# A third Strassen pair in the first MLP product of a two-layer encoder, with four conversion buffers and another order of the conversions

## The chip, the cores and the metric

The kernel runs on one core of a Trainium2 chip. The metric is the device time of one execution in microseconds. The engines are named as the profile names them: PE is TensorE (matmuls; PEld its weight loads), DVE is VectorE, ACT is ScalarE, POOL is GpSimd, SP is SyncE, which here issues the weight loads from memory.

## The reference

A trunk of two layers on 256 rows of width 2048, in float32. Each layer is an attention half (two kinds of attention, gated and merged) and an MLP half; the change touches the MLP half and, through one rule of order, the products in front of it.

```
for l in range(DEPTH):                                   # DEPTH = 2
    u = rmsnorm(x, norm_mix[l]);  proj = u @ w_in[l]     # 2048 x 8256
    ...                                                  # MLA and neighbourhood attention, gates
    x = x + merged @ w_out[l]                            # 2048 x 2048
    h = rmsnorm(x, norm_mlp[l]) @ w_ff1[l]               # 2048 x 8192
    x = x + jnp.square(jax.nn.relu(h)) @ w_ff2[l]        # 8192 x 2048
return rmsnorm(x, norm_final)
```

## The kernel before, in words

**Precision by halves.** Every float32 operand of a large product is cut in two: `hi` is a copy in the format that the matmuls take (float32r), made by ACT, and `lo` is the source minus `hi`, made by DVE (`parts`, lines 173 to 179). A product is then three matmuls: hi x hi, hi x lo, lo x hi. For weights this is work for each 1 MB piece that is loaded; for the activations it is done once, and the two parts lie in slots (`pair`).

**A product call, `gemm_s`.** It multiplies the 256 x 2048 activations by 1024 columns of a weight matrix. The 2048 rows are cut into 8 *row pairs* of 256 rows. For each, SP loads one raw tile `raw` (128 x 2048, three buffers), and a pair is either *plain* or *Strassen*. A plain pair is 8 products of three 128x512 matmuls, with one conversion of 2048 columns. A Strassen pair is 7 products of three (in Winograd's form): DVE first builds four sums of the weights' blocks (`sums`, lines 465, 468, 469), then three raw blocks (1536 columns) and the four sums (2048 columns) are converted. The activations need four sums too (`sums_of`, lines 364 to 367), made once for each pair that is Strassen. The results of the products stand in eight PSUM banks; at the end of a call DVE adds them up into four result tiles (line 476, the evacuation) and calls `evac`.

**What is Strassen where.** `MIXED` and `MERGED` name the pairs of the gate products and of the output product (1, 2, 3, visited in the order 0, 4, 1, 5, 2, 6, 3, 7), `FIRST` those of the first MLP product, `SECOND` those of the second (both visited from 0 to 7).

**The MLP half.** It runs in four blocks of 2048 hidden columns. A block is two calls of the first product (`w_ff1`), whose results go through ReLU, 16 transposes and a square into new activations (`turned_pair`, lines 391 to 413), and two calls of the second (`w_ff2`), whose results POOL adds into `x` by accumulating DMAs (line 870); the last block has one such call, and its other half by plain products (`gemm_a`). So there are 16 calls of the first product and 14 of the second in the two layers. The transposes and conversions of new activations are generators that are advanced by ticks between the products of the next call; `drain()`, at a call's first Strassen pair, finishes all of them.

**What sets the order.** A scheduler orders each engine's instructions when the program is built, by its own model of time; each engine then works strictly in that order, and waits where an input or a free buffer is late. The tile pools set which buffers there are: `raws` (3), `hi` and `lo` (3 each in the MLP half, 8 KB a partition), `sums` (1), and 52 slots of 2 KB for activations and results.

Of the kernel before, what the change touches and what calls it, by code (L numbers as in the profile page):

```python
# [33 lines left out]
F32 = mybir.dt.float32  # L34
F32R = mybir.dt.float32r
AF = mybir.ActivationFunctionType
ALU = mybir.AluOpType
AX = mybir.AxisListType

P = 128  # L40
S = 256
# [17 lines left out]

NSLOT, SMALL, RBUFS, HBUFS = 52, 8, 3, 4


FIRST, SECOND = (3, 5), (2, 4, 6)


MIXED, MERGED = (1, 2, 3), (1, 2, 3)
# [7 lines left out]
def trunk(ctx: ExitStack, tc: tile.TileContext, x, w_in, w_uq, w_ukv, rpb, w_o_mla, w_o_na,  # L76
          w_out, w_ff1, w_ff2, gains, gain_fin, cos, sin, turns, halves, mask, out):
    nc = tc.nc
    const = ctx.enter_context(tc.tile_pool(name="const", bufs=1))
    slots = ctx.enter_context(tc.tile_pool(name="slots", bufs=NSLOT))  # L80
    keep = ctx.enter_context(tc.tile_pool(name="keep", bufs=2))
    raws = ctx.enter_context(tc.tile_pool(name="raws", bufs=RBUFS))
    psum = ctx.enter_context(tc.tile_pool(name="psum", bufs=8, space=bass.MemoryType.PSUM))

    tmp = wpool = spool = None
    hbufs, smalls, strips = HBUFS, SMALL, False

    def bank():
        return psum.tile([P, 512], F32, tag="bank", name="bank", bufs=8)
# [7 lines left out]
    def wide():  # L97
        return slots.tile([P, 512], F32, tag="slot", name="wide")
# [30 lines left out]
    def tick():  # L129
        clock[0] += 1  # L130
        for i, (ready, gen) in enumerate(pending):
            if ready <= clock[0]:
                advance(i)
                return
        if queued and clock[0] - clock[1] >= SPACING:
            clock[1] = clock[0]
            pending.append((clock[0], queued.pop(0)))
            advance(len(pending) - 1)
# [9 lines left out]
    def drain():  # L148
        while pending or queued:
            if pending:  # L150
                clock[0] = max(clock[0], pending[0][0])
            tick()
# [20 lines left out]
    def parts(src):  # L173

        hi, lo = (wpool.tile([P, 2048 if strips else 1024], F32R, tag=tag, name=tag,
                             bufs=3 if strips else hbufs)[:, :src.shape[-1]] for tag in ("hi", "lo"))
        nc.scalar.copy(hi, src)  # L177
        nc.vector.tensor_tensor(lo, src, hi.bitcast(F32), op=ALU.subtract)  # L178
        return hi, lo
# [109 lines left out]

    def rows_of(col):  # L290

        dg = [keep.tile([P, P], F32, tag="diag", name="diag", bufs=4) for _ in range(2)]
        for t in range(2):
            nc.vector.tensor_scalar_mul(dg[t], ident, col[:, t:t + 1])
        yield 8
        pb = abank()
        for t in range(2):
            nc.tensor.matmul(pb[:, t * P:(t + 1) * P], ones, dg[t], start=True, stop=True)
        row = keep.tile([P, S], F32, tag="rrow", name="rrow", bufs=4)
        nc.vector.tensor_copy(row, pb[:, :S])  # L300
        return row

# [7 lines left out]
    class Norm:  # L310
# [5 lines left out]
        def add(self, t):  # L316
            if self.acc is None:
                self.acc = tmp.tile([P, S], F32, tag="acc", name="acc", bufs=2)
                nc.scalar.activation(self.acc, t, AF.Square)
                return  # L320
            sq = small()
            nc.scalar.activation(sq, t, AF.Square)
            nc.vector.tensor_tensor(self.acc, self.acc, sq, op=ALU.add)

        def scales(self):

            ps = abank()
            for t in range(2):
                nc.tensor.matmul(ps[:, 2 * t:2 * t + 2], self.acc[:, t * P:(t + 1) * P], ones[:, :2],
                                 start=True, stop=True)  # L330
            v = keep.tile([P, 2], F32, tag="var", name="var", bufs=2)
            nc.vector.tensor_copy(v, ps[:, 0:4:2])
            self.col = root(v, self.width, "col")
            self.row = yield from rows_of(self.col)
# [80 lines left out]
    def gemm_s(w, c0, get, order, pairs, evac):  # L415

        b, count, total = {}, {}, {i: 0 for i in range(1, 9)}
        for j in order:  # L420
            for i in (range(1, 8) if j in pairs else (2, 3, 4, 8)):
                total[i] += 3 if j in pairs else 6

        def mm(i, x, y):
            if i not in b:
                b[i], count[i] = bank(), 0
            count[i] += 1
            nc.tensor.matmul(b[i], x, y, start=count[i] == 1, stop=count[i] == total[i])  # L428

        def products(*todo):  # L430
            for n, (i, ah, al, wh, wl) in enumerate(todo):
                mm(i, ah, wh)
                mm(i, al, wh)
                if n % 2:
                    tick()
            for i, ah, al, wh, wl in todo:
                mm(i, ah, wl)

        def cut(src):
            out, step = [], 2048 if strips else 1024  # L440
            for c in range(0, src.shape[-1], step):
                hi, lo = parts(src[:, c:min(c + step, src.shape[-1])])
                out += [(hi[:, i:i + 512], lo[:, i:i + 512]) for i in range(0, hi.shape[-1], 512)]
            return out

        first = next(j for j in order if j in pairs)
        for j in order:
            raw = raws.tile([P, 2048], F32, tag="raw", name="raw", bufs=RBUFS)
            nc.sync.dma_start(raw.rearrange("p (k n) -> p k n", n=1024),
                              w[2 * j * P:(2 * j + 2) * P, c0:c0 + 1024].rearrange("(k p) n -> p k n", p=P))  # L450
            if j not in pairs:
                ws = cut(raw)
                ah, al = get(j)
                products(*((i, ah[2 * k + t], al[2 * k + t], *ws[2 * k + side])
                           for k in range(2) for i, t, side in ((2, 0, 1), (3, 0, 0), (4, 1, 1), (8, 1, 0))))
                continue
            if j == first:
                drain()
            if strips:
                whole_ts = spool.tile([P, 2048], F32, tag="sums", name="sums", bufs=1)  # L460
                ts = whole_ts[:, :1024], whole_ts[:, 1024:]
            else:
                ts = [tmp.tile([P, 1024], F32, tag="pp", name="sums", bufs=2) for _ in range(2)]
            t1, t3, t2, t4 = (s[:, i:i + 512] for s in ts for i in range(0, 1024, 512))
            nc.vector.tensor_tensor(ts[0].rearrange("p (a n) -> p a n", a=2),  # L465
                                    raw[:, :512].rearrange("p (a n) -> p a n", a=1).to_broadcast([P, 2, 512]),
                                    raw[:, 512:1536].rearrange("p (a n) -> p a n", a=2), op=ALU.subtract)
            nc.vector.tensor_tensor(t2, raw[:, 1024:1536], t1, op=ALU.subtract)
            nc.vector.tensor_tensor(t4, raw[:, 1536:], t2, op=ALU.subtract)  # L469
            w11, w22, w21 = cut(raw[:, 512:])  # L470
            w1, w3, w2, w4 = cut(whole_ts) if strips else cut(ts[0]) + cut(ts[1])
            (a11, _, a12, a22, s1, s2, s3, s4), (l11, _, l12, l22, r1, r2, r3, r4) = get(j)
            products((1, a11, l11, *w11), (2, a12, l12, *w21), (3, s4, r4, *w22), (5, s1, r1, *w1),
                     (7, s3, r3, *w3), (6, s2, r2, *w2), (4, a22, l22, *w4))
        r11, r22, r12, r21 = (wide() for _ in range(4))
        add = lambda o, a, c: nc.vector.tensor_tensor(o, a, c, op=ALU.add)  # L476
        nc.scalar.copy(r11, b[1])
        add(r22, r11, b[6])
        add(r12, r22, b[5])
        add(r21, r22, b[7])  # L480
        add(r22, r21, b[5])
        add(r12, r12, b[3])
        add(r11, r11, b[2])
        add(r22, r22, b[8])
        add(r21, r21, b[4])
        evac({(0, 1): r11, (0, 0): r12, (1, 1): r21, (1, 0): r22})
# [171 lines left out]
    for l in range(DEPTH):  # L658
        half_a = ExitStack()
        hbufs, smalls, strips = HBUFS, SMALL, False  # L660
        wpool = half_a.enter_context(tc.tile_pool(name="wpool", bufs=4, reuse_waits="tile"))
        tmp = half_a.enter_context(tc.tile_pool(name="tmp", bufs=2, reuse_waits="tile"))
# [67 lines left out]

        mixed = blocks(xg, xs4, MIXED)
        gemm_s(wi, C_GB, mixed, ORDER, MIXED, gate(part, 0))
        local(0)
        local(1)
        gemm_s(wi, C_GB + 1024, mixed, ORDER, MIXED, gate(part, 1))
        for g in range(2):
            gemm_s(wi, C_GA + g * 1024, mixed, ORDER, MIXED, gate(other, g))
# [63 lines left out]
        last = l == DEPTH - 1  # L801
        half_b = ExitStack()
        strips = True
        spool = half_b.enter_context(tc.tile_pool(name="spool", bufs=1, reuse_waits="tile"))
        wpool = half_b.enter_context(tc.tile_pool(name="wpool2", bufs=4, reuse_waits="tile"))
        tmp = half_b.enter_context(tc.tile_pool(name="tmp2", bufs=2, reuse_waits="tile"))
        mlp = RowNorm()
# [151 lines left out]
```

## Time and profile before

| | |
|---|---|
| median of 3 runs | 2630.33 us (2630.33 to 2630.65) |
| profiled execution | 2630.92 us, its span 2629.1 us |
| granted PE clock, mean | 0.998 |
| PE / PEld busy | 2599.1 us (99%) / 2183.3 us (83%) |
| DVE / ACT / POOL busy | 2116.7 us (81%) / 1457.8 us (55%) / 97.2 us (4%) |
| read from HBM | 492.18 MB |

A time with the span's start as zero is called by its microsecond: the first layer's MLP half runs from 626.7 on. "Busy" of a row is the union of its instructions' times, "idle before" the time its engine stood still just ahead of them, with what ended it. In a timeline, neighbours of one line are merged, and the idle time stands in brackets.

### The profile page before, as it was taken

The numbers are of one execution on the slowest core, as the hardware profiler recorded it, in microseconds if no ns is written. First come the engines' busy times: TensorE is split into PE (matmuls) and PEld (weight loads), VectorE is DVE, ScalarE is ACT, GpSimd is POOL, SyncE is SP. The second block draws the span as 40 slices with busy tenths as digits, with TensorE's granted clock in tenths as the row PEclk, the third lists the DMA queues.
The fourth block names the chain that finished last, engine by engine and source line by source line (L and its number), as shares of the span: only waits on it lengthen the run. The fifth ranks groups of instructions, "written<-read, shape, count | busy, mean of one in ns | idle before, by whom it ended". The sixth has DMA issues, their size and how long they took to land.

```text
span 2629.1 us, 32272 instructions
## 1 busy us (share of the span) xinstructions
PE 2599.1 (99%) x12498; PEld 2183.3 (83%) x12498; DVE 2116.7 (81%) x2496; ACT 1457.8 (55%) x1719; POOL 97.2 (4%) x117
## 2 busy tenths in 40 slices
PE   8999999999999999999999999999999999999998
PEld 7888888878888888888888888888788888888886
DVE  6678789789888888888667787896998888888885
ACT  6555556546655545546545555564566555455553
POOL 1100000000000010000001000000000000100000
PEclk9999999999999999999999999999999999999999
DMA  7555555555567485675565555644555765756744
GB/s 243 182 159 192 192 195 170 162 179 192 200 198 242 160 244 199 199 241 178 190 195 174 173 180 190 207 146 160 188 196 192 217 210 195 244 196 198 259 160 148
DMA packets 175258, 508.97 MB, mean 194 GB/s; under 512 B 13696, under 2 KB 18176, under 8 KB 175104
## 3 DMA queue, kind: packets, MB, share of 16 engines
q1 hardware_dynamic: 166192, 490.08, 55.7%
q0 software_dynamic: 8768, 16.78, 3.3%
q8 instruction: 98, 1.61, 0.2%
q14 instruction: 56, 0.46, 0.1%
q10 hardware_dynamic: 144, 0.04, 0.0%
HBM read 492.18 MB, written 2.10 MB: 188 GB/s over the span
## 4 chain that ended last, share of the span: by engine, by line
PE 76%; issue 19%; DVE 2%; ACT 1%; POOL 1%; DMA 0%; SPq 0%; POOLq 0%; DVEq 0%; ACTq 0%
PE bank L428 47%; PE bank L244 8%; PE bank L279 7%; PE bank L248 4%; PE bank L283 3%; PE bank L223 1%; PE bank L398 1%; DVE lo L178 1%; PE bank L252 1%; PE bank L224 1%; PE bank L254 1%; PE bank L253 1%; POOL xt L870 1%; PE bank L558 0%; ACT hi L177 0%
## 5 line engine op out<-in xcount | busy, mean ns | idle before, releaser
L428 PE MATMUL bank<-hi,pair 128*128 128x512 f32 x5156 | 1269.8, 390 | 7.0 <-ACT hi L177 6.2
L428 PEld LDWEIGHTS bank<-hi,pair 128*128 128x128 f32 x5156 | 964.9, 188 | 210.6 <-ACT hi L177 9.9
L177 ACT CAST hi<-raw 128x2048 fp32r<-128x2048 f32 (+3 forms) x416 | 630.0, 1534 | 449.1 <-PE bank L428 323.0
L178 DVE TENSOR_TENSOR lo<-raw,hi 128x2048 fp32r<-128x2048 f32 (+3 forms) x416 | 751.0, 1817 | 94.7 <-ACT hi L177 61.5
L428 PE MATMUL bank<-lo,pair 128*128 128x512 f32 x2578 | 677.4, 389 | 0.0
L428 PEld LDWEIGHTS bank<-lo,pair 128*128 128x128 f32 x2578 | 483.7, 188 | 100.2
L178 DVE TENSOR_TENSOR lo<-sums,hi 128x2048 fp32r<-128x2048 f32 (+1 forms) x134 | 254.6, 1909 | 176.3 <-ACT hi L177 118.5
L177 ACT CAST hi<-sums 128x2048 fp32r<-128x2048 f32 (+1 forms) x134 | 214.8, 1603 | 290.3 <-DVE sums L469 187.4
L202 DVE TENSOR_TENSOR lo<-raw,hi 128x1024 fp32r<-128x1024 f32 (+1 forms) x224 | 268.7, 1205 | 121.9 <-ACT hi L201 114.2
L201 ACT CAST hi<-raw 128x1024 fp32r<-128x1024 f32 (+1 forms) x224 | 230.0, 1036 | 208.6 <-PE bank L279 84.8
L244 PE MATMUL bank<-hi,pair 128*128 128x512 f32 x1024 | 259.6, 390 | 0.0
L244 PEld LDWEIGHTS bank<-hi,pair 128*128 128x128 f32 x1024 | 190.6, 188 | 38.9
L476 DVE TENSOR_TENSOR wide<-wide,bank 128x512 f32<-128x512 f32 x336 | 216.1, 680 | 4.5 <-PE bank L428 4.1
L279 PE MATMUL bank<-pair,hi 128*128 128x512 f32 x768 | 203.2, 397 | 4.5 <-ACT hi L201 3.2
L279 PEld LDWEIGHTS bank<-pair,hi 128*128 128x128 f32 x768 | 136.3, 190 | 26.9 <-ACT hi L201 3.6
L248 PE MATMUL bank<-lo,pair 128*128 128x512 f32 x512 | 142.8, 392 | 0.0
L465 DVE TENSOR_TENSOR sums<-raw 128x1024 f32<-128x1024 f32 x110 | 134.1, 1219 | 5.7 <-DMA raw<-in_w_ff 5.1
L283 PEld LDWEIGHTS bank<-pair,lo 128*128 128x128 f32 x768 | 106.9, 190 | 8.7
L283 PE MATMUL bank<-pair,lo 128*128 128x256 f32 x768 | 111.6, 283 | 0.0
L248 PEld LDWEIGHTS bank<-lo,pair 128*128 128x128 f32 x512 | 95.2, 188 | 18.9
L408 DVE TENSOR_TENSOR pair<-wide,pair 128x512 fp32r<-128x512 f32 x108 | 72.4, 686 | 13.9 <-ACT pair L407 13.9
L870 POOL DMA_DIRECT2D xt<-wide x48 | 42.3, 968 | 977.0 <-DVE wide L476 702.6
(131 smaller groups left out, 1727.8 us busy)
## 6 DMA issues: line engine op xcount, KB each, us to landing
raw<-in_w_ff SPq DMA_DIRECT2D x256, 1024.0 KB, 5.2
raw<-in_w_in SPq DMA_DIRECT2D x124, 1024.0 KB, 5.1
raw<-in_w_out SPq DMA_DIRECT2D x32, 1024.0 KB, 5.3
raw<-in_w_o_na SPq DMA_DIRECT2D x16, 1024.0 KB, 5.0
raw<-in_w_o_mla SPq DMA_DIRECT2D x16, 1024.0 KB, 5.0
xt<-wide POOLq DMA_DIRECT2D x48, 256.0 KB, 6.8
raw<-in_w_ukv SPq DMA_DIRECT2D x8, 1024.0 KB, 5.6
raw<-in_w_uq SPq DMA_DIRECT2D x8, 768.0 KB, 4.6
```

What stands on the lines that cost most here:

```text
L177: nc.scalar.copy(hi, src)
L178: nc.vector.tensor_tensor(lo, src, hi.bitcast(F32), op=ALU.subtract)
L201: nc.scalar.copy(hi, src)
L202: nc.vector.tensor_tensor(lo, src, hi.bitcast(F32), op=ALU.subtract)
L244: nc.tensor.matmul(ps[t], a, wh[:, k], start=k0 + k + i == 0, stop=False)
L248: nc.tensor.matmul(ps[t], sides(have(acts, k0 + k), t)[0], wl[:, k], start=False, stop=k0 + k == nk - 1)
L279: nc.tensor.matmul(ps[m], wh[:, k, m * P:(m + 1) * P], have(acts, k0 + k), start=k0 + k == 0, stop=False)
L283: nc.tensor.matmul(ps[m][:, :S], wl[:, k, m * P:(m + 1) * P], have(acts, k0 + k)[:, :S], start=False, stop=k0 + k == nk - 1)
L408: nc.vector.tensor_tensor(lw, src, h.bitcast(F32), op=ALU.subtract)
L428: nc.tensor.matmul(b[i], x, y, start=count[i] == 1, stop=count[i] == total[i])
L465: nc.vector.tensor_tensor(ts[0].rearrange("p (a n) -> p a n", a=2), raw[:, :512].rearrange("p (a n) -> p a n", a=1).to_broadcast([P, 2, 512]),
L476: add = lambda o, a, c: nc.vector.tensor_tensor(o, a, c, op=ALU.add)
```

## The change

It does these things:

- `FIRST` goes from (3, 5) to (2, 4, 6): three of the eight row pairs of each first-product call are Strassen. The activations' sums are then made for pairs 2, 4 and 6.
- `hi` and `lo` have four buffers each in the MLP half instead of three, and `sums` moves from a pool of its own into theirs.
- The conversion of a Strassen pair's raw blocks is issued behind the last of the sums (`tc.issue_after`), in all products.
- To make room, one slot goes (51), two small tiles (`diag`, `rrow`) move from a lasting pool to the halves' own, and the scratch for POOL's DMAs is halved.

```diff
-NSLOT, SMALL, RBUFS, HBUFS = 52, 8, 3, 4
-FIRST, SECOND = (3, 5), (2, 4, 6)
+NSLOT, SMALL, RBUFS, HBUFS = 51, 8, 3, 4
+FIRST, SECOND = (2, 4, 6), (2, 4, 6)
...
         hi, lo = (wpool.tile([P, 2048 if strips else 1024], F32R, tag=tag, name=tag,
-                             bufs=3 if strips else hbufs)[:, :src.shape[-1]] for tag in ("hi", "lo"))
+                             bufs=hbufs)[:, :src.shape[-1]] for tag in ("hi", "lo"))
...
-        dg = [keep.tile([P, P], F32, tag="diag", name="diag", bufs=4) for _ in range(2)]
+        dg = [tmp.tile([P, P], F32, tag="diag", name="diag", bufs=4) for _ in range(2)]
...
-        row = keep.tile([P, S], F32, tag="rrow", name="rrow", bufs=4)
+        row = tmp.tile([P, S], F32, tag="rrow", name="rrow", bufs=4)
...
-                whole_ts = spool.tile([P, 2048], F32, tag="sums", name="sums", bufs=1)
+                whole_ts = wpool.tile([P, 2048], F32, tag="sums", name="sums", bufs=1)
...
-            nc.vector.tensor_tensor(t4, raw[:, 1536:], t2, op=ALU.subtract)
-            w11, w22, w21 = cut(raw[:, 512:])
+            final = nc.vector.tensor_tensor(t4, raw[:, 1536:], t2, op=ALU.subtract)
+            with tc.issue_after(final.ins):
+                w11, w22, w21 = cut(raw[:, 512:])
...
-        spool = half_b.enter_context(tc.tile_pool(name="spool", bufs=1, reuse_waits="tile"))
...
-    nc = bacc.Bacc("TRN2", target_bir_lowering=False, num_devices=1, dynamic_dma_scratch_size=8192)
+    nc = bacc.Bacc("TRN2", target_bir_lowering=False, num_devices=1, dynamic_dma_scratch_size=4096)
```

In the program's order, PE has 48 matmuls of 128x512 fewer (32 with a hi of the weights, 16 with a lo). DVE has 16 more of each of the three sums, 16 conversions of 2048 raw columns fewer, 16 of 1536 and 16 of the sums more, and in each layer one more set of the activations' sums and its lo; ACT's conversions change alike. The orders of SP and POOL are the same. From line 470 on, the lines of the changed kernel are one higher, so its evacuation is L477.

First place: DVE in the first call of the first product in the second MLP block of layer 0 (the call at 800.30). Before, from the middle of its first Strassen pair (`sums_7206`, pair 3) through its second (`sums_7275`, pair 5); `lo_7246` is pair 4:

```order
L468 TENSOR_TENSOR sums_7206<-raw_7204,sums_7206 128x512
L469 TENSOR_TENSOR sums_7206<-raw_7204,sums_7206 128x512
L178 TENSOR_TENSOR lo_7211<-raw_7204,hi_7210 128x1536
L178 TENSOR_TENSOR lo_7215<-sums_7206,hi_7214 128x2048
L465 TENSOR_TENSOR sums_7275<-raw_7273 128x1024
L178 TENSOR_TENSOR lo_7246<-raw_7243,hi_7245 128x2048
L468 TENSOR_TENSOR sums_7275<-raw_7273,sums_7275 128x512
L178 TENSOR_TENSOR lo_7280<-raw_7273,hi_7279 128x1536
L469 TENSOR_TENSOR sums_7275<-raw_7273,sums_7275 128x512
L178 TENSOR_TENSOR lo_7284<-sums_7275,hi_7283 128x2048
```

The same stretch now, from the end of pair 2's sums (`sums_7192`) through pair 4's (`sums_7261`); `lo_7232` is pair 3:

```order
L469 TENSOR_TENSOR sums_7192<-raw_7190,sums_7192 128x512
L178 TENSOR_TENSOR lo_7197<-raw_7190,hi_7196 128x1536
L477 TENSOR_TENSOR wide_7110<-wide_7110,bank_6861 128x512
L477 TENSOR_TENSOR wide_7112<-wide_7112,bank_6858 128x512
L178 TENSOR_TENSOR lo_7201<-sums_7192,hi_7200 128x2048
L465 TENSOR_TENSOR sums_7261<-raw_7259 128x1024
L178 TENSOR_TENSOR lo_7232<-raw_7229,hi_7231 128x2048
L468 TENSOR_TENSOR sums_7261<-raw_7259,sums_7261 128x512
L469 TENSOR_TENSOR sums_7261<-raw_7259,sums_7261 128x512
L178 TENSOR_TENSOR lo_7266<-raw_7259,hi_7265 128x1536
L178 TENSOR_TENSOR lo_7270<-sums_7261,hi_7269 128x2048
```

The raw lo (1536 columns) of the second Strassen pair stood between its sums and now stands behind the last of them; the first Strassen pair comes one plain pair earlier, so the last two additions of the call before (L477) now stand between its two conversions.

Second place: DVE at the opening of layer 0's MLP, the first call of the first product (the call at 626.70), around the residual additions into `xt` that the transposes of the activations wait for. Before, with `sums_5981` the first Strassen pair:

```order
L465 TENSOR_TENSOR sums_5981<-raw_5979 128x1024
L825 TENSOR_TENSOR xt0_87<-xt0_87,wide_5797 128x512
L825 TENSOR_TENSOR xt0_87<-xt0_87,wide_5799 128x512
L476 TENSOR_TENSOR wide_5798<-wide_5798,bank_5492 128x512
L476 TENSOR_TENSOR wide_5800<-wide_5800,bank_5489 128x512
L468 TENSOR_TENSOR sums_5981<-raw_5979,sums_5981 128x512
L825 TENSOR_TENSOR xt1_88<-xt1_88,wide_5798 128x512
L178 TENSOR_TENSOR lo_5986<-raw_5979,hi_5985 128x1536
L825 TENSOR_TENSOR xt1_88<-xt1_88,wide_5800 128x512
L469 TENSOR_TENSOR sums_5981<-raw_5979,sums_5981 128x512
```

Now, with `sums_5957`:

```order
L468 TENSOR_TENSOR sums_5957<-raw_5955,sums_5957 128x512
L825 TENSOR_TENSOR xt0_87<-xt0_87,wide_5794 128x512
L825 TENSOR_TENSOR xt0_87<-xt0_87,wide_5796 128x512
L477 TENSOR_TENSOR wide_5795<-wide_5795,bank_5489 128x512
L477 TENSOR_TENSOR wide_5797<-wide_5797,bank_5486 128x512
L469 TENSOR_TENSOR sums_5957<-raw_5955,sums_5957 128x512
L178 TENSOR_TENSOR lo_5962<-raw_5955,hi_5961 128x1536
L825 TENSOR_TENSOR xt1_88<-xt1_88,wide_5795 128x512
L825 TENSOR_TENSOR xt1_88<-xt1_88,wide_5797 128x512
L178 TENSOR_TENSOR lo_5966<-sums_5957,hi_5965 128x2048
```

The last sum (L469) moved ahead of the raw lo and ahead of the second pair of residual additions, which now stand behind both.

More of the change, by code (lines that the diff above doesn't have):

```diff
@@ L83, in trunk @@
     psum = ctx.enter_context(tc.tile_pool(name="psum", bufs=8, space=bass.MemoryType.PSUM))
-    tmp = wpool = spool = None
+    tmp = wpool = None
     hbufs, smalls, strips = HBUFS, SMALL, False
```

## The prediction

> **What bounds the kernel now.** I read the page first: the busy shares, the granted clock, and the chain that ended last.
>
> ```profile
> span 2629.1 us, 32272 instructions
> PE 2599.1 (99%) x12498; PEld 2183.3 (83%) x12498; DVE 2116.7 (81%) x2496; ACT 1457.8 (55%) x1719; POOL 97.2 (4%) x117
> PEclk9999999999999999999999999999999999999999
> PE 76%; issue 19%; DVE 2%; ACT 1%; POOL 1%; DMA 0%; SPq 0%; POOLq 0%; DVEq 0%; ACTq 0%
> ```
>
> TensorE (PE) is busy for 99% of the span at full clock, and the chain is PE and its issue for 95%. A busy PE is not yet PE at its pace, so I read the pace from the timeline, at the end of the second first-product call of the first MLP block, columns: start, duration, then the instructions merged.
>
> ```profile
> 710.14 3.79 PE L428 MATMUL bank<-hi,pair 128*128 128x512 f32 x16
> 713.77 1.98 PE L428 MATMUL bank<-lo,pair 128*128 128x512 f32 x8
> 715.58 0.62 PE L428 MATMUL bank<-hi,pair 128*128 128x512 f32 x2
> ```
>
> From 710.14 to 713.77 there are 16 matmuls, from 713.77 to 715.58 eight: 0.227 us and 0.226 us each. I use 0.227. The weights' conversion is what could break this pace, so I cut the layer at its matrix-product calls; the columns are the stretch, its length, then busy time (instructions) of PE, PEld, DVE, ACT, POOL, clock, DMA share, GB/s.
>
> ```profile
> 539.40:583.50 44.10, 43.13 (x192) 35.15 (x193) 40.64 (x40) 24.13 (x20) 0.00 (x0) 1.00 0.60 190
> 583.50:626.70 43.20, 43.20 (x200) 36.03 (x199) 41.34 (x42) 28.33 (x34) 0.00 (x0) 1.00 0.61 204
> 626.70:671.70 45.00, 44.73 (x204) 36.36 (x203) 39.24 (x43) 27.96 (x33) 0.69 (x1) 1.00 0.55 190
> 671.70:715.60 43.90, 43.90 (x204) 36.59 (x203) 37.71 (x37) 26.31 (x25) 0.00 (x0) 1.00 0.64 213
> 715.60:758.80 43.20, 43.20 (x200) 36.04 (x199) 35.70 (x37) 26.62 (x25) 0.00 (x0) 1.00 0.49 160
> 758.80:800.30 41.50, 41.50 (x184) 34.35 (x183) 35.16 (x29) 19.61 (x12) 3.59 (x4) 1.00 0.77 236
> 800.30:842.50 42.20, 42.20 (x188) 34.94 (x187) 34.64 (x30) 20.41 (x12) 3.55 (x4) 1.00 0.80 255
> 842.50:886.40 43.90, 43.90 (x204) 36.59 (x202) 36.08 (x35) 26.19 (x25) 0.00 (x0) 1.00 0.54 187
> ```
>
> The first two are the two calls of the attention's output product, then come first product (two calls), second product (two calls), and the next block's first product (two calls). The first-product call at 800.30 has 186 matmuls and takes 42.20 us; the second-product call before it has three Strassen pairs, so 183 matmuls, and takes 41.50 us. Both are their matmul counts times 0.227 us (42.2 and 41.5): nothing waits. The calls with 43.2 and 43.9 carry 16 transposes more, 1.7 us or 0.11 each. So PE sets the time call by call, and one call already runs in the form the change gives the first product. Only the stretch at 626.70 is longer than its like (45.00 against 43.90): 1.1 us of waiting at the opening of a layer's MLP. The waits of PE from 530 to 720 us name it, and the waits of a whole steady stretch (758.8 to 971.1) show what the converters wait for (total us, times, longest):
>
> ```profile
> PE bank L428 <- ACT hi L177: 2.0, 2, 1.1
> PE bank L428 <- ACT pair L407: 0.3, 1, 0.3
> ...
> ACT hi L177 <- DVE sums L469: 42.9, 9, 6.4
> ACT hi L177 <- PE bank L428: 39.6, 22, 7.3
> DVE lo L178 <- ACT hi L177: 26.6, 15, 2.5
> ```
>
> In the steady stretch PE has no row among the waiters; ScalarE (ACT) and VectorE (DVE) wait for each other and for PE to free buffers.
>
> **The change part by part.** Durations, one row for each form (busy us in total, mean ns of one, idle before):
>
> ```profile
> L178 DVE TENSOR_TENSOR lo<-raw,hi 128x2048 fp32r<-128x2048 f32 x202 | 459.9, 2286 | 55.8 <-ACT hi L177 39.1 <-PE bank L428 11.5 <-ACT pair L166 3.9
> L177 ACT CAST hi<-raw 128x2048 fp32r<-128x2048 f32 x202 | 383.7, 1913 | 203.3 <-PE bank L428 142.3 <-DMA raw<-in_w_ff 35.0 <-PE bank L244 16.0
> L178 DVE TENSOR_TENSOR lo<-sums,hi 128x2048 fp32r<-128x2048 f32 x86 | 197.1, 2292 | 140.2 <-ACT hi L177 118.0 <-PE bank L428 22.1
> L177 ACT CAST hi<-sums 128x2048 fp32r<-128x2048 f32 x86 | 164.3, 1911 | 233.2 <-DVE sums L469 183.5 <-PE bank L428 49.7
> L178 DVE TENSOR_TENSOR lo<-raw,hi 128x1536 fp32r<-128x1536 f32 x86 | 150.8, 1754 | 18.2 <-ACT hi L177 11.7 <-PE bank L428 5.7
> L465 DVE TENSOR_TENSOR sums<-raw 128x1024 f32<-128x1024 f32 x110 | 134.1, 1219 | 5.7 <-DMA raw<-in_w_ff 5.1 <-DMA raw<-in_w_in 0.3
> L177 ACT CAST hi<-raw 128x1536 fp32r<-128x1536 f32 x86 | 127.6, 1484 | 161.7 <-PE bank L428 129.1 <-DMA raw<-in_w_ff 24.4 <-DMA raw<-in_w_out 6.4
> L469 DVE TENSOR_TENSOR sums<-raw,sums 128x512 f32<-128x512 f32 x110 | 75.4, 685 | 0.8
> L468 DVE TENSOR_TENSOR sums<-raw,sums 128x512 f32<-128x512 f32 x110 | 75.2, 684 | 0.1
> L408 DVE TENSOR_TENSOR pair<-wide,pair 128x512 fp32r<-128x512 f32 x108 | 72.4, 686 | 13.9 <-ACT pair L407 13.9
> L364 DVE TENSOR_TENSOR wide<-wide 128x128 f32<-128x128 f32 x40 | 11.3, 283 | 0.0
> ```
>
> *The third Strassen pair.* A plain pair is 8 products of 3 matmuls, a Strassen pair 7 of 3. Two layers x four blocks x two calls = 16 calls lose 3 matmuls each: 48 x 0.227 = 10.9 us off PE, all of it on the path. (By the two calls compared above: 16 x 0.70 = 11.2, the same within the windows' edges.)
>
> [...]
>
> What the pair adds: on DVE 1219 + 684 + 685 + 1754 + 2292 in place of 2286 = 4.35 us a call by durations. Neighbours overlap a little on DVE:
>
> ```profile
> 843.48 1.88 DVE L476 TENSOR_TENSOR wide<-wide,bank 128x512 f32<-128x512 f32 x3
> ```
>
> Three of about 0.68 us take 1.88, so one instruction more costs some 0.08 us less than its duration; with four more that is 4.0 us a call, 64 us in all. On ACT 1484 + 1911 - 1913 = 1.5 us a call. Where does it lie? A steady block (715.6 to 886.4) has 35.70 + 35.16 + 34.64 + 36.08 = 141.6 us of DVE in 170.8; it gets 149.6 in 169.4, 88%. Its fullest first-product call goes from 36.08 to 40.1 of 43.2. ACT stays near 28 of 43. I price this at nothing: the cover is PE's own stream. If the cover fails, each call can show up to the 4.0 us (ACT's 1.5 runs beside it).
>
> *The opening of a layer's MLP.* There the cover is thin. The call at 626.70 has 39.24 us of DVE, gets the 4.0 and one more Strassen form of the activations (4 x 0.28 + 0.69 = 1.8 by durations, about 1.4 by pitch; of the three pairs two now fall in this call): 44.6 against 45.00 - 0.7 = 44.3. The call before has 41.34 of 43.20, the call after goes to 41.7 of 43.2. So DVE falls behind by a fraction and catches up later. From above: 4.0 + 1.4 = 5.4 us a layer if all of it shows. From below: -1.1 if the present wait goes, since the fourth buffer lets conversion run ahead. It is nearest to its own ledger, 44.6 - 44.3 = 0.3, and I take 0.5 a layer, +1.0 in all.
>
> *Four buffers.* hi and lo are allocated one chunk of 2048 further ahead, which the rows of ACT waiting for a PE bank bear on: 39.6 us in the steady stretch, none of it on PE's path. It gains only where PE waits: the first output-product call (44.10, with 8 transposes of 0.11 us it should take 42.4, so 1.7 us) and the opening. From -1.7 to +1.7 a layer; I take 0, as nothing in that call's amount of work changes.
>
> *Raw lo behind the sums.* The last sum and then ACT's hi of the sums come one 1.75 us conversion earlier; the raw lo comes 1.4 us later (L468, L469). PE uses the raw lo only after 14 products with hi, 3.2 us into the pair, and today it is not waited for. The raw buffer is freed when both the last sum and the raw lo are done, the same total as before. What hangs on it is the next load on SyncE's queue:
>
> ```profile
> raw<-in_w_ff SPq DMA_DIRECT2D x256, 1024.0 KB, 5.2
> xt<-wide POOLq DMA_DIRECT2D x48, 256.0 KB, 6.8
> ...
> SPq L449 <- DVE lo L178: 158.6, 32, 13.1
> ```
>
> SyncE waits for lo in any case; a load lands 5.2 us after issue, a pair lasts 4.8 to 5.4 us on PE, and three raw buffers give some 15 us. Cost 0.
>
> *Memory paid for it.* 51 slots for 52 while the third pair holds two more: the activations' 22, the hidden's 22 and a result's 4 make 48, so 3 are left where 6 were; a turned pair wants two for a moment. The scratch for GpSimd's DMAs is halved; its accumulating DMAs land in 6.8 us and come four to a call of over 41 us. The rows moved to the tmp pool change no instruction. All 0, at worst a wait of the order of the 1.1 us above at a few places.
>
> Sum: -10.9 + 1.0 = -9.9 us. The profiled run took 2630.92 with a span of 2629.1, so 2621.0 for it; the median 2630.33 lies 0.6 lower, which gives 2620.4.
>
> **The rivals.**
>
> *DVE becomes the bound in the first product.* DVE works in order; behind a waiting evacuation (L476) stand the next lo, the sums for ACT, and through them PE. In a steady block DVE idles 29.2 us now; if those idles (ACT's hi, banks not yet complete) cannot shrink, the added 4.0 us a call show on PE. It is slower than now from 0.68 us of PE waiting a call (10.9/16), by over 0.2% from 1.0 us. At half, 2.0 a call: 2630.3 - 10.9 + 32 = 2651. For it: 93% in the fullest call. Against it: the output call at 583.50 runs with 41.34 of 43.20 and no wait, and the second product has the form already. Chance 0.08.
>
> *The openings eat the gain.* The full 5.4 us a layer: 2630.3 - 10.9 + 10.8 = 2630, no change; a half leaves -5.5, the edge of 0.2%. For it: the one wait today is there. Chance 0.11 for within 0.2%, 0.07 for a smaller gain that still counts.
>
> *The waits of today go too.* Fourth buffer and order remove 1.1 and 1.7 a layer: 2630.3 - 10.9 - 5.6 = 2613.8. The first wait of the output product is for a first conversion that no buffer hurries, so 0.08.
>
> *Something else spaces PE's stream,* such as the weight loads, and a matmul less saves only that.
>
> ```profile
> L428 PEld LDWEIGHTS bank<-hi,pair 128*128 128x128 f32 x5156 | 964.9, 188 | 210.6 <-ACT hi L177 9.9 <-ACT pair L407 1.4 <-DVE pair L408 0.8
> ```
>
> At 188 ns the 48 bring 9.0 us: 2622.3. Against it: the two compared calls differ by 0.70 us for 3 matmuls, not by 0.56. Chance 0.01. [...]
>
> *The change doesn't do what it says:* the program's order has 48 products fewer on PE, and the sums ahead of the raw lo; no chance left for that.
>
> **How the numbers follow.** The forecast case has 0.65, its own range 2618 to 2624. What a measurement can tell from no change is about 0.2%, 5.3 us. Faster: 0.65 + 0.07 + 0.08 + 0.01 = 0.81; same: 0.11; slower: 0.08. The range 2616 to 2627 leaves out the DVE-bound case (0.08), most of the openings' case (0.07) and part of the best case (0.04).
>
> **What would show it.** PE's L428 rows have 5124 and 2562 matmuls, at the same mean. Each later first-product call is 0.7 us shorter (41.5, 43.2) with no wait row of PE; DVE's busy total is some 65 us higher and its share near 83 to 84%. A row of PE waiting for L177 or L408 in the later blocks would show the DVE rival; stretches over 45 us at each layer's opening the second. Wrong would be above all a first product at 42.2 or more with DVE near 100% of it.

## The result and the profile after

The changed kernel takes 2616.69 us (median of 4 runs, 2615.81 to 2617.43), the kernel before in the same comparison 2630.33 (2630.01 to 2630.65): a ratio of 0.9948 with a 95% interval of 0.9931 to 0.9965, so 13.6 us less where 9.9 were forecast. The page of its profiled execution (2616.59 us):

```profile
span 2614.8 us, 32295 instructions
PE 2588.5 (99%) x12450; PEld 2173.8 (83%) x12450; DVE 2183.3 (83%) x2570; ACT 1483.6 (57%) x1737; POOL 101.2 (4%) x117
PE 88%; issue 8%; DVE 2%; ACT 1%; DMA 0%; POOL 0%; SPq 0%; POOLq 0%; DVEq 0%; ACTq 0%
L428 PE MATMUL bank<-hi,pair 128*128 128x512 f32 x5124 | 1284.2, 390 | 4.1 <-ACT hi L177 3.9
```

There are 48 matmuls fewer (12450 against 12498), DVE is busy for 66.6 us more, and a matmul's mean is as before. The windows below are the same eight calls as in the prediction (output product twice, then two first-product and two second-product calls, then the next block's first product):

```profile
538.80:581.30 42.50, 42.50 (x191) 35.29 (x192) 42.10 (x42) 25.14 (x21) 0.00 (x0) 1.00 0.64 208
581.30:624.60 43.30, 43.30 (x200) 36.00 (x199) 40.34 (x42) 27.99 (x34) 0.00 (x0) 1.00 0.58 196
624.60:668.70 44.10, 43.96 (x201) 35.85 (x201) 41.61 (x50) 28.23 (x34) 2.93 (x1) 1.00 0.52 181
668.70:711.90 43.20, 43.20 (x200) 36.03 (x199) 40.68 (x38) 28.47 (x26) 0.00 (x0) 1.00 0.62 206
711.90:755.30 43.40, 43.40 (x201) 35.99 (x200) 38.38 (x44) 26.99 (x26) 0.00 (x0) 1.00 0.56 179
755.30:796.80 41.50, 41.50 (x185) 34.37 (x184) 39.17 (x32) 21.32 (x13) 3.66 (x4) 1.00 0.87 277
796.80:838.20 41.40, 41.40 (x184) 34.30 (x183) 36.04 (x30) 20.37 (x13) 3.54 (x4) 1.00 0.74 226
838.20:881.50 43.30, 43.30 (x200) 35.96 (x199) 38.25 (x37) 27.60 (x25) 0.00 (x0) 1.00 0.57 192
```

The later first-product calls go from 42.2 to 41.4 or 41.5 and from 43.9 to 43.3, as the count of matmuls says. Two stretches gain that were not meant to: the first output-product call (44.1 to 42.5) and the MLP's opening (45.0 to 44.1). The calls' lengths by the starts of the matmuls, both layers added, give the account: output product -2.9, openings -1.9, the 14 other first-product calls -0.59 to -0.68 each or -9.0, the second product's calls +0.7 in all. That is -13.1 of the 14.3 between the two profiled executions; the rest is spread.

PE's waits from 528 to 720 us, and what the converters wait for in the steady stretch (755.3 to 966.3):

```profile
PE bank L428 <- ACT hi L177: 0.8, 1, 0.8
```
```profile
ACT hi L177 <- DVE sums L469: 37.8, 10, 4.9
ACT hi L177 <- PE bank L428: 21.4, 15, 3.3
```

Of PE's two waits before (2.0 us), the one of 1.13 us at 539.40, ahead of the output product's first matmul, is still there with 0.81 at 538.79, and the one of 0.82 at 563.86 is gone. ACT waits for a bank 21.4 us where it was 39.6. The wait that went is seen in the output product, here before the change; a timeline's columns are start, duration, instruction, and the idle time ahead of it:

```profile
557.03 1.22 DVE L465 TENSOR_TENSOR sums<-raw 128x1024 f32<-128x1024 f32 x1
558.17 1.75 DVE L178 TENSOR_TENSOR lo<-raw,hi 128x1536 fp32r<-128x1536 f32 x1
560.17 0.68 DVE L468 TENSOR_TENSOR sums<-raw,sums 128x512 f32<-128x512 f32 x1
561.10 0.68 DVE L469 TENSOR_TENSOR sums<-raw,sums 128x512 f32<-128x512 f32 x1
561.89 1.91 ACT L177 CAST hi<-sums 128x2048 fp32r<-128x2048 f32 x1 [0.95 <-DVE sums L469]
563.86 4.37 PE L428 MATMUL bank<-hi,pair 128*128 128x512 f32 x16 [0.82 <-ACT hi L177]
```

and after it:

```profile
555.13 1.22 DVE L465 TENSOR_TENSOR sums<-raw 128x1024 f32<-128x1024 f32 x1
556.60 0.68 DVE L468 TENSOR_TENSOR sums<-raw,sums 128x512 f32<-128x512 f32 x1
557.53 0.68 DVE L469 TENSOR_TENSOR sums<-raw,sums 128x512 f32<-128x512 f32 x1
558.13 1.75 DVE L178 TENSOR_TENSOR lo<-raw,hi 128x1536 fp32r<-128x1536 f32 x1
558.32 1.92 ACT L177 CAST hi<-sums 128x2048 fp32r<-128x2048 f32 x1 [0.95 <-DVE sums L469]
```

PE's wait hangs on a chain through three engines: DVE's last sum (L469), ACT's `hi` of the sums, PE. Before, the raw `lo` of 1.75 us stood inside this chain. Now L469 starts 2.40 us behind the start of L465 instead of 4.07, the `hi` starts 3.19 behind it instead of 4.86, and PE has no wait there. That the order alone does this, and not the buffers, is what the experiments have to show.

### The profile page after: what moved, and what is told of

Read it like the earlier page. It is cut to its first block, busy times and chain, and to the rows that moved or that the text cites. A ratio compares the mean times of both kernels' runs of the same rounds, so it can differ in the third digit from the quotient of the medians.

```text
span 2614.8 us, 32295 instructions
## 1 busy us (share of the span) xinstructions
PE 2588.5 (99%) x12450; PEld 2173.8 (83%) x12450; DVE 2183.3 (83%) x2570; ACT 1483.6 (57%) x1737; POOL 101.2 (4%) x117
## 4 chain that ended last, share of the span: by engine, by line
PE 88%; issue 8%; DVE 2%; ACT 1%; DMA 0%; POOL 0%; SPq 0%; POOLq 0%; DVEq 0%; ACTq 0%
PE bank L428 59%; PE bank L244 8%; PE bank L279 7%; PE bank L248 4%; PE bank L283 3%; PE bank L223 2%; PE bank L398 1%; PE bank L224 1%; PE bank L252 1%; PE bank L254 1%; PE bank L253 1%; DVE lo L178 1%; PE bank L559 1%; PE bank L496 0%; ACT hi L177 0%
## 5 line engine op out<-in xcount | busy, mean ns | idle before, releaser
L428 PE MATMUL bank<-hi,pair 128*128 128x512 f32 x5124 | 1284.2, 390 | 4.1 <-ACT hi L177 3.9
L428 PEld LDWEIGHTS bank<-hi,pair 128*128 128x128 f32 x5124 | 958.0, 188 | 204.8 <-ACT hi L177 5.6
L178 DVE TENSOR_TENSOR lo<-raw,hi 128x2048 fp32r<-128x2048 f32 (+3 forms) x416 | 741.8, 1796 | 77.3 <-ACT hi L177 50.9
L177 ACT CAST hi<-raw 128x2048 fp32r<-128x2048 f32 (+3 forms) x416 | 622.8, 1517 | 307.5 <-PE bank L428 163.3
L428 PE MATMUL bank<-lo,pair 128*128 128x512 f32 x2562 | 697.6, 390 | 0.0
L428 PEld LDWEIGHTS bank<-lo,pair 128*128 128x128 f32 x2562 | 479.7, 188 | 99.3
L177 ACT CAST hi<-sums 128x2048 fp32r<-128x2048 f32 (+1 forms) x150 | 244.9, 1638 | 292.3 <-DVE sums L469 167.8
L178 DVE TENSOR_TENSOR lo<-sums,hi 128x2048 fp32r<-128x2048 f32 (+1 forms) x150 | 290.8, 1947 | 98.6 <-ACT hi L177 58.7
L244 PE MATMUL bank<-hi,pair 128*128 128x512 f32 x1024 | 261.0, 391 | 0.0
L477 DVE TENSOR_TENSOR wide<-wide,bank 128x512 f32<-128x512 f32 x336 | 214.9, 679 | 6.5 <-PE bank L428 6.4
L465 DVE TENSOR_TENSOR sums<-raw 128x1024 f32<-128x1024 f32 x126 | 153.6, 1219 | 6.2 <-DMA raw<-in_w_ff 4.8
L248 PE MATMUL bank<-lo,pair 128*128 128x512 f32 x512 | 141.6, 391 | 0.0
L407 ACT CAST pair<-wide 128x512 fp32r<-128x512 f32 x110 | 68.2, 620 | 56.8 <-DVE wide L366 54.5
L469 DVE TENSOR_TENSOR sums<-raw,sums 128x512 f32<-128x512 f32 x126 | 86.6, 687 | 2.1
```

The source lines that it names most:

```text
L244: nc.tensor.matmul(ps[t], a, wh[:, k], start=k0 + k + i == 0, stop=False)
L248: nc.tensor.matmul(ps[t], sides(have(acts, k0 + k), t)[0], wl[:, k], start=False, stop=k0 + k == nk - 1)
L469: final = nc.vector.tensor_tensor(t4, raw[:, 1536:], t2, op=ALU.subtract)
```

## The experiments

The theories: A, the saved matmuls and the order each bring their part, whatever else is done; B, the fourth buffer carries the gain; C, the order is the condition on which the third pair and the buffers pay at all. For each run the ratio is to the kernel before, with its 95% interval.

**The third pair alone** (before, with one line changed):

```diff
-FIRST, SECOND = (3, 5), (2, 4, 6)
+FIRST, SECOND = (2, 4, 6), (2, 4, 6)
```

> The kernel before with only FIRST = (2, 4, 6): three hi and lo buffers, raw lo where the scheduler puts it. Theory A (the gain is 10.9 us of matmuls plus 3.2 us of waits in the output product that the new order of the conversions takes away; the fourth buffer brings little by itself): the 48 matmuls go and little else, 2619 to 2621 us, each later first-product call 41.5 and 43.3 us, the first output-product call still 44.1 us. Theory B (the fourth buffer is what lets the third pair pay): the first product waits for its hi with three buffers, 0.3 us a call or more, so 2624 us or more. Theory C (the order is what lets it pay): the same as B here.

Measured: 2639.66 us, 1.0036 [1.0024, 1.0049]: 9.2 us slower, with 48 matmuls fewer. That misses theory A's 2619 to 2621 us and fits the 2624 or more of B and C. The steady first-product calls do shorten (42.16 to 41.48), but the openings grow to 48.6 and 47.8 us, the first second-product call of each block from 43.25 to 44.0, and the second output call from 43.2 to 44.1. At the opening:

```profile
646.29 0.68 DVE L468 TENSOR_TENSOR sums<-raw,sums 128x512 f32<-128x512 f32 x1
...
647.19 1.76 DVE L178 TENSOR_TENSOR lo<-raw,hi 128x1536 fp32r<-128x1536 f32 x1
...
648.86 0.68 DVE L469 TENSOR_TENSOR sums<-raw,sums 128x512 f32<-128x512 f32 x1
...
649.64 1.90 ACT L177 CAST hi<-sums 128x2048 fp32r<-128x2048 f32 x1 [2.48 <-DVE sums L469]
...
651.59 1.01 PE L428 MATMUL bank<-hi,pair 128*128 128x512 f32 x3 [1.86 <-ACT hi L177]
```

ACT stood idle for 2.48 us for L469, of which 1.76 are the raw `lo` ahead of it, and PE 1.86 for ACT. Two windows show what came on top of this wait (first the wait with what lies around it, then the 3.4 us behind it):

```profile
649.20:652.60 3.40, 1.54 (x5) 0.58 (x4) 1.58 (x3) 2.96 (x4) 0.29 (x1) 1.00 0.55 148
652.60:656.00 3.40, 3.15 (x8) 2.48 (x9) 3.40 (x4) 2.36 (x6) 0.00 (x0) 0.50 0.39 160
```

The granted clock (ahead of the DMA share and the GB/s: 1.00, then 0.50) is halved for 3.4 us, and the matmuls stand 0.427 us apart there instead of 0.227.

**The order alone** (before, with the raw conversion behind the last sum):

```diff
-            nc.vector.tensor_tensor(t4, raw[:, 1536:], t2, op=ALU.subtract)
-            w11, w22, w21 = cut(raw[:, 512:])
+            final = nc.vector.tensor_tensor(t4, raw[:, 1536:], t2, op=ALU.subtract)
+            with tc.issue_after(final.ins):
+                w11, w22, w21 = cut(raw[:, 512:])
```

> The kernel before with only the raw lo issued behind the last sum. Theory A: the first output-product call of each layer falls from 44.1 to 42.5 us, nothing else moves: 2627.2 us. Theory B: the call keeps its 44.1 us, 2630 us.

Measured: 2625.69 us, 0.9981 [0.9972, 0.9990], 4.8 us faster with no matmul less:

```profile
539.00:581.50 42.50, 42.50 (x192) 35.26 (x193) 40.77 (x40) 24.33 (x20) 0.00 (x0) 1.00 0.63 201
624.80:668.80 44.00, 44.00 (x204) 36.44 (x203) 39.08 (x43) 27.39 (x33) 1.06 (x1) 1.00 0.54 185
```

The first output call has its 42.5 us and the opening its 44.0 from the order alone, with three buffers; the other calls are nearly as before. By the starts of the matmuls the first layer gains 1.6 and 0.9 us and the second 1.4 and 0.9: 4.7 of the 4.8. Theory A had the output call right and had not expected the opening to move. There PE's wait before was another one: at 649.67 a matmul starts 0.66 us behind the last, 0.27 of it idle for the new activations (ACT's `pair`, L407). With the order this wait is gone; through which of the moved instructions was not followed.

**The buffers alone, and with the order.** The first is the kernel before with four buffers and the memory edits that pay for them; the second is the changed kernel with the pairs of before (order and buffers):

```diff
-FIRST, SECOND = (2, 4, 6), (2, 4, 6)
+FIRST, SECOND = (3, 5), (2, 4, 6)
```

> The kernel before with only the four buffers and what pays for them (51 slots, moved tiles, half the scratch). Theory A: nothing moves, 2630 us, the first output-product call at 44 us. Theory B: the call falls to 42.5 us, 2627 us. If the memory paid for it costs something, this kernel shows it alone: above 2630.3 us.

> The changed kernel with FIRST back at (3, 5): four buffers and the new order, without the third pair. Theory A: 2616.7 + 10.9 = 2627.6 us, with the first output-product call at 42.5 us. If the third pair adds waits of its own, this one is less than 10.9 us slower than the changed kernel.

Measured: the buffers alone 2641.67 us, 1.0043 [1.0030, 1.0056], 11.2 us slower; with the order 2625.13, 0.9979 [0.9970, 0.9988]. The two differ in the order alone and the memory edits are in both, so these cost nothing that shows, and the loss of the first hangs on the order; neither theory had expected it. The second is 8.4 us slower than the changed kernel, less than the 10.9 of its matmuls, so the third pair does lose something elsewhere. Both output calls and the opening of the buffers alone, then a stretch of its output product:

```profile
538.20:583.60 45.40, 43.72 (x191) 34.94 (x192) 40.22 (x41) 23.91 (x20) 0.00 (x0) 1.00 0.56 179
583.60:629.30 45.70, 43.68 (x201) 35.86 (x200) 41.21 (x41) 27.80 (x33) 0.00 (x0) 1.00 0.55 187
629.30:676.40 47.10, 44.99 (x204) 36.20 (x203) 39.47 (x43) 28.77 (x33) 3.48 (x1) 1.00 0.59 202
```
```profile
567.62 1.22 DVE L465 TENSOR_TENSOR sums<-raw 128x1024 f32<-128x1024 f32 x1
568.75 1.75 DVE L178 TENSOR_TENSOR lo<-raw,hi 128x1536 fp32r<-128x1536 f32 x1
571.36 0.68 DVE L468 TENSOR_TENSOR sums<-raw,sums 128x512 f32<-128x512 f32 x1
572.07 0.69 DVE L469 TENSOR_TENSOR sums<-raw,sums 128x512 f32<-128x512 f32 x1
572.85 0.59 ACT L477 COPY wide<-bank 128x512 f32<-128x512 f32 x1 [5.71 <-PE bank L428]
573.33 1.91 ACT L177 CAST hi<-sums 128x2048 fp32r<-128x2048 f32 x1
575.29 4.86 PE L428 MATMUL bank<-hi,pair 128*128 128x512 f32 x20 [0.44 <-ACT hi L177]
```

The raw `lo` stands ahead of both late sums. A count over DVE's traces gives how often the raw `lo` of 1536 columns (output product and MLP) starts ahead of its pair's last sum: 44 of 86 times before, 64 of 86 with four buffers, 79 of 102 with the third pair alone, never where the order is set. So with the extra buffer the scheduler placed the raw `lo` earlier more often, against the chain that PE waits for. The raw `lo` isn't the whole of it. Here the `hi` of the sums also stands behind ACT's copy of a PSUM bank (L477), which ACT could start only when PE had added the bank's last product (its idle time ahead of the copy, 5.71 us, ends with PE's L428); at the longest wait, PE's 2.02 us at 620.96 in the second output call, the last sum ends at 617.79, this copy starts at 618.53 and the `hi` at 619.01. Before, and in both versions with the order set and two pairs, the copy stands behind this `hi`. The runs show that the one edit of the order takes the whole loss away; how it is shared between the two places was not tried.

**The changed kernel without the order** (third pair and buffers):

```diff
-            final = nc.vector.tensor_tensor(t4, raw[:, 1536:], t2, op=ALU.subtract)
-            with tc.issue_after(final.ins):
-                w11, w22, w21 = cut(raw[:, 512:])
+            nc.vector.tensor_tensor(t4, raw[:, 1536:], t2, op=ALU.subtract)
+            w11, w22, w21 = cut(raw[:, 512:])
```

> The changed kernel without the new order: third pair and four buffers, raw lo where the scheduler puts it. After the first four experiments theory C (the order is what lets the third pair and the fourth buffer pay, since without it conversions that are not urgent stand on VectorE ahead of the sums that ScalarE and PE wait for) expects the losses of the third pair alone (9.2 us over the kernel before) and of the buffers alone (11.2) to stay: 2640 us or more, with waits at each layer's opening and in the steady blocks. Theory B (the fourth buffer lets it pay) expects the steady blocks free of waits and 2625 us or less.

Measured: 2663.59 us, 1.0126 [1.0110, 1.0142], 33 us slower than before and 47 slower than the changed kernel, from this one edit, as theory C expected (2640 or more). The count is 93 of 102. PE's waits over the whole run, and a place in a second-product call, which the edit to the first product doesn't touch:

```profile
PE bank L428 <- ACT hi L177: 18.3, 22, 2.0
PE bank L428 <- ACT pair L407: 13.8, 9, 1.6
```
```profile
908.65 1.75 DVE L178 TENSOR_TENSOR lo<-raw,hi 128x1536 fp32r<-128x1536 f32 x1
...
912.13 0.68 DVE L469 TENSOR_TENSOR sums<-raw,sums 128x512 f32<-128x512 f32 x1
912.90 1.91 ACT L177 CAST hi<-sums 128x2048 fp32r<-128x2048 f32 x1 [5.50 <-DVE sums L469]
...
917.17 0.51 PE L428 MATMUL bank<-hi,pair 128*128 128x512 f32 x1 [1.58 <-ACT pair L407]
```

ACT waits 5.5 us for L469, and the new activations (`pair`, L407), which stand behind that `hi` and one more on ACT, come late for PE. Six times the clock halves for 3.4 us or longer; its mean over the run is 0.994, before 0.998.

**The third pair and the order with three buffers** (both edits above on the kernel before):

> The kernel before with the third pair and the new order, three buffers, no memory moved. Theory C: close to the changed kernel, 2616 to 2619 us. Theory B: the steady blocks wait with three buffers as they do with the third pair alone (43.6 and 44.05 us for the two calls with transposes in place of 43.3), so some 1 us a block, 2624 us or more.

Measured: 2624.15 us, 0.9975 [0.9966, 0.9984]: 7.5 us short of the changed kernel, and only 1.5 better than the order alone, with runs of both that overlap. So theory C's 2616 to 2619 us is missed, and theory B's 2624 or more is met. ACT's wait for a buffer that PE holds, in the steady stretch:

```profile
ACT hi L177 <- PE bank L428: 48.0, 29, 7.6
```

48.0 us where the changed kernel has 21.4. The steady calls of the first product have their 41.5 and 43.3, but the openings take 45.2 (44.0 and 43.9 in the changed kernel) and the first second-product call of a block 43.85 for 43.3. So the fourth buffer is worth 7.5 us once the third pair and the order are there, nothing that shows with the order alone (0.6, with runs that overlap), and -11.2 without the order. The table puts the eight combinations together (medians, us; the column of four buffers has the memory edits too):

| | three buffers | four buffers |
|---|---|---|
| two pairs, order of before | 2630.33 | 2641.67 |
| two pairs, sums first | 2625.69 | 2625.13 |
| three pairs, order of before | 2639.66 | 2663.59 |
| three pairs, sums first | 2624.15 | 2616.69 |

Theory A falls. Theory C holds as far as the sign goes: in the rows with the old order each of the other two edits costs time, and in those with the sums first none does. But the order isn't enough by itself, and there theory B has its part: with the sums first the third pair brings 8.4 us with four buffers and 1.5 with three. The gain of 13.6 takes all three edits: 5.2 come with order and buffers and 8.4 with the third pair on top.

**A fourth pair.** If PE's matmul count sets the steady calls, another pair should bring 0.68 us a call. Three versions of the changed kernel make pair 0 Strassen too, visited after pair 1: in all first-product calls of blocks 1 to 3, in the first call of these blocks alone, and the last with the activations' sums of pair 0 formed later. This is the first; the second has `more = b and g == 0`:

```diff
-FIRST, SECOND = (2, 4, 6), (2, 4, 6)
+FIRST, SECOND = (0, 2, 4, 6), (2, 4, 6)
...
-                gemm_s(w_ff1[l], b * D + g * 1024, lambda j: have(xg, j), range(8), FIRST, relu2)
+                more = b
+                gemm_s(w_ff1[l], b * D + g * 1024, lambda j: have(xg, j) if more or j else tuple(v[:4] for v in have(xg, j)),
+                       [1, 0, 3, 2, 5, 4, 7, 6] if more else range(8), FIRST if more else FIRST[1:], relu2)
```

> The changed kernel with a fourth Strassen pair (pair 0) in the first product of blocks 1 to 3, pairs visited as 1, 0, 3, 2, 5, 4, 7, 6 there: 12 calls lose 3 matmuls more, 36 x 0.227 = 8.2 us. VectorE's share of a steady block rises from 151.8 us of 169.6 to about 160 of 168. If PE still sets the pace, 2616.7 - 8.2 + 1 (the activations' sums of pair 0) = 2609 us. If VectorE is the bound from here on, the two calls with transposes exceed 43.3 us and it is 2617 us or slower.

> As with four pairs, but in the first of the two first-product calls of a block only: 6 calls, 4.1 us fewer on PE, VectorE at about 156 of 169 us in a block. If PE still sets the pace: 2613.5 us. If VectorE is the bound: 2617 us or slower.

Measured: 2642.38 us, 1.0045 [1.0031, 1.0059], and 2634.40, 1.0013 [1.0004, 1.0022], both slower than the kernel before and far from the 2609 and 2613.5 of a PE that sets the pace. Of the second, the opening, a later call with four pairs, and a stretch of the opening:

```profile
624.70:678.50 53.80, 47.01 (x200) 36.57 (x199) 46.51 (x51) 29.65 (x36) 4.27 (x1) 0.97 0.49 165
...
806.70:847.50 40.80, 40.80 (x182) 33.78 (x181) 37.56 (x28) 22.39 (x14) 3.55 (x4) 1.00 0.80 236
```
```profile
655.40 0.62 ACT L407 CAST pair<-wide 128x512 fp32r<-128x512 f32 x1 [3.78 <-DVE wide L366]
656.07 0.56 PE L428 MATMUL bank<-hi,pair 128*128 128x512 f32 x1 [3.40 <-ACT pair L407]
```

The four-pair call takes 40.8 us, 180 x 0.227, as the count says. But both versions made the activations' sums of pair 0 at the opening, with those of the other pairs, though no call uses them before block 1: DVE has 46.5 us to do there for 41.6, the activations come late, PE waits 3.4 us at one place and 1.7 at another, the clock is 0.50 for 3.4 us behind the longer one, and the opening takes 9.8 us more. With four pairs in both calls of a block (the first version) there is a second price: the second-product call behind them grows from 43.3 to 45.4 or 45.9 us (in the last block from 44.2 to 46.3), and PE waits 1.47 us for DVE's `pair` (L408) once in each of these six calls. The third version leaves `FIRST` at (2, 4, 6), names pair 0 `MORE`, and forms the four sums of pair 0 in block 0's last second-product call, where DVE has room (39.17 us of 41.50 in the changed kernel):

```diff
-                gemm_s(w_ff1[l], b * D + g * 1024, lambda j: have(xg, j), range(8), FIRST, relu2)
+                more = b and g == 0
+                gemm_s(w_ff1[l], b * D + g * 1024, lambda j: have(xg, j),
+                       [1, 0, 3, 2, 5, 4, 7, 6] if more else range(8), (MORE, *FIRST) if more else FIRST, relu2)
...
+                if b == 0 and g == 1:
+                    start(summed(held[0], xg, MORE), 8)
```

> Four pairs in the first of the two first-product calls of blocks 1 to 3, as in the kernel before this one, but the activations' sums of pair 0 are formed in block 0's last second-product call instead of in the layer's opening. If the loss of that kernel (first call of a layer 53.8 us against 44.0) came from those sums at the opening, the opening is back at 44 us, the six calls stay at 40.8 us, and the time is 2616.7 - 4.1 = 2612.6 us plus up to 1 us. If the loss came from the fourth pair or the slots it takes, the openings or the steady blocks still wait: 2617 us or more.

> The changed kernel once more, to stand beside the last one on the same chip: 2616.7 us, within 1 us.

Measured on one chip: 2612.46 us (2611.90 to 2613.13), 0.9930 [0.9918, 0.9942], and the changed kernel beside it 2616.43 (2615.69 to 2616.68), 0.9945 [0.9931, 0.9958]. The intervals overlap, the two sets of five times do not. The third version's opening, the call that makes the sums, and a four-pair call:

```profile
625.00:669.10 44.10, 43.95 (x201) 35.85 (x201) 41.61 (x50) 28.10 (x34) 2.93 (x1) 1.00 0.53 181
...
755.70:797.10 41.40, 41.40 (x184) 34.32 (x183) 38.90 (x36) 20.15 (x14) 3.66 (x4) 1.00 0.84 259
797.10:837.90 40.80, 40.80 (x181) 33.80 (x181) 38.32 (x28) 23.07 (x14) 3.54 (x4) 1.00 0.77 235
```

The opening is that of the changed kernel, and six calls of 0.68 less make 4.1, against 4.0 measured, so the loss was those sums' place at the opening. It beats both kernels.

## Why the prediction was right, and where it was not

The time lies in the range, 3.7 us below the forecast and 0.7 above the range's lower end; the forecast case's own range, 2618 to 2624, it misses. The terms came out unequally. The third pair with its opening was to bring 9.9 us and everything else nothing; order, buffers and memory edits together brought 5.2, and the third pair on top of them 8.4. That the two errors have opposite signs, and the sum lands so near, is luck.

- *The third pair, -10.9 on PE.* Right, in the form the calls have now: against the version with order and buffers but two pairs, each of the 14 later calls is 0.59 to 0.68 us shorter, 9.0 in all, and no wait of PE appears there. The full 0.68 for three matmuls is 0.227 us each, which also speaks against the rival of 188 ns. By itself, on the order of before, the same edit costs 9.2 us; the cover "PE's own stream" was there only because the order came with it.
- *The opening, +1.0.* The size was right against the right base. With order and buffers the openings take 44.04 with two pairs and 44.02 and 43.92 with three, so most of the 0.68 saved is lost again, 1.2 in both layers. Against the kernel before it gains 0.9 a layer, which the order brings alone. My reading of the rows was wrong here: the wait of 1.1 us that I took for the opening's is the one at 539.40, ahead of the output product, and the opening's only row was the 0.3 us for `pair`.
- *Raw lo behind the sums: "Cost 0".* This is the step that failed. It measured -4.8 alone, and it decides the sign of the other two. I had named the 1.75 us by which the last sum and ACT's `hi` come earlier, and quoted PE's wait for that `hi`, but then looked only at who waits for the raw `lo` and at SP's queue. I didn't ask which instruction the wait of PE goes back to. I had held the first output call's 1.7 us to be the wait for a first conversion; the timeline shows the `hi` of a later pair's sums, and the wait for the first conversion lies ahead of the call's first matmul (1.13 us with three buffers, 0.81 with four).
- *Four buffers: 0, from -1.7 to +1.7 a layer.* The size depends on the rest: 0 holds with the order alone (0.6 gained, with runs that overlap), but 7.5 are gained with order and third pair and 11.2 lost without the order, outside those bounds. I had read ACT's 39.6 us of waits for a bank as slack; with a third pair's conversions they are not.
- *Memory: 0.* Nothing speaks against it: order, buffers and memory edits together are no slower than the order alone.
- *The rivals.* "The waits of today go too" (2613.8, chance 0.08) is the nearest in mechanism: they went for the most part, but by the order, where I had argued from a first conversion that no buffer hurries. "DVE becomes the bound" was built on DVE's share of a call. In the runs where it seemed to come true (third pair alone, buffers alone, both without the order), DVE was busy for 40.2 us of 45.4 in the output call of the buffers alone, while the changed kernel's output call has 42.10 of 42.50 and runs without a wait; what made PE wait was which of DVE's and ACT's instructions stood first.
- *How much a wait costs.* The row at 563.86 says 0.82 us, the call lost 1.6. The matmuls' starts there are 1.21, 0.34, 0.54 and 0.33 us apart where 0.227 is the pace: 1.5 us. The idle time of a row counts from the end of the matmul before, which is 0.16 us later than its slot (0.389 us of duration at a pace of 0.227), and leaves out the slow start behind the wait.

## What to carry to other kernels

Follow each wait of the bounding engine back through the engines before it, and take everything off that chain that needn't be on it, before work is added or buffers are: here one reordering was worth 4.8 us alone and 47 us with the other edits in place. More buffers are no safe gift to a scheduler that fills them by its own model of time; fix the order of the chain first. And where activations are prepared for several calls, do in the crowded opening only what its own calls use.

## What was not expected of the hardware

A wait of PE of about 2 us was followed by a halved clock in one run and not in another. With the third pair alone, matmul starts lay 2.25 us apart at 651.59, and from 652.6 on the clock was 0.50 for 3.4 us, which costs an estimated 1.7 us more at most (half of the 3.4); it happened once in each layer's opening. The 3.4 us ahead of the fall (649.20 to 652.60) held 1.54 us of matmuls. The changed kernel without the order had six such places; the kernel before and the changed one have none in the two layers: their clock stands at 1.00 in one stretch, from 12.5 to 2620.3 us before and from 13.4 to 2607.5 after.

A wait of 2.02 us with four buffers alone (at 620.96) brought no fall: the clock is 1.00 from 583.60 to 629.30. By its timeline the 3.4 us ahead of 620.96 held 1.38 us of matmuls, less than the 1.54, so neither a wait of this length nor so few matmuls in 3.4 us is enough for a fall. What else it takes was not shown; no run moved a wait.
